# ScalarE copies the whole accumulator of an MLP feature block, and VectorE adds its halves in SBUF

## The chip, the core and the metric

The kernel runs on one NeuronCore of a Trainium2 chip. The metric is device time in microseconds (us) of one execution. Five engines work in parallel, each through its own instruction stream in order: TensorE (PE in the profile; its weight loads stand apart as PEld), VectorE (DVE), ScalarE (ACT), GpSimd (POOL) and SyncE (SP), which here issues the DMAs. They wait for one another by semaphores. Matmuls write to PSUM, which has eight banks of 512 f32 per partition; everything else lies in SBUF.

## The reference, cut to what matters

Two decoder layers over 256 tokens of width 2048, each with a mixer and a squared-ReLU MLP of width 8192, all in f32:

```python
def squared_relu_mlp(h, w1, w2):
    return jnp.square(jax.nn.relu(h @ w1)) @ w2

for layer in range(DEPTH):            # DEPTH = 2
    h = rms_norm(x, norm_mix[layer])
    x = x + mixer(h)                  # layer 0: MLA and mLSTM; layer 1: dilated attention
    x = x + squared_relu_mlp(rms_norm(x, norm_mlp[layer]), mlp_w1[layer], mlp_w2[layer])
return rms_norm(x, norm_final)
```

The change touches the middle of the MLP: the values of `h @ w1` on their way from PSUM to the ReLU.

## The kernel before, in words

**Three products for one.** Every f32 operand is split into a high part `hi` in the matmul format f32r and a low part `lo`, the rest. A product is `hi*hi + hi*lo + lo*hi`. Weights come by DMA in pieces of 512 KB (`load`, L118 to L128) and are split in `halves` (L130): ScalarE rounds them to `wh` (L135), VectorE subtracts to `wl` (L136). There are four raw buffers, four `wh` and four `wl`.

**Feature blocks.** In the first MLP product (`mm_feats`, L158) the weights are the stationary operand and the activations move. A tile `T` holds its two parts side by side, 256 tokens of `hi` and 256 of `lo`. So one matmul over 512 columns (L164) gives `wh*hi` in the left half of a PSUM bank and `wh*lo` in the right half, and a second one over 256 columns (L168) adds `wl*hi` to the left half. At the end of a feature block (128 features, 16 + 16 matmuls) the two halves of the bank have to be added. That is what `both` does (L282 to L286): ScalarE copies the right half to an SBUF tile `bt`, then VectorE adds it to the left half, which it reads from PSUM. Only when VectorE has read it is the bank free.

**After the sum.** `evac_h` (L1021) goes on from `both`: ScalarE applies ReLU (L1028) and squares (L1030 or L1039). For the first ten blocks of a quarter (`c < SEVEN`, `c` counting pairs) the squares of a pair of blocks go to a tile `hp`, VectorE makes three sums of it (L1041 to L1043), and ScalarE and VectorE split that into `pt` (L1045, L1046), the operand of a product scheme with seven multiplications for eight. For the other six, `ht` is split by `split_to` (L300, L301).

**The order of the MLP.** The 8192 features go in four quarters of 16 blocks. The first eight blocks of a layer run in pairs and rotate through the four accumulator banks. The other 56 run one at a time, all of them in bank 3 (`blocks`, L1083, `bank=3`, `kt=8`), so a block can't begin before the block before it has left the bank. To bridge that, `woven` (L443) puts steps of the second MLP product between the blocks: ten steps of `steps_seven`, alternately `go_a` (9 matmuls of 512 columns, L215) and `go_b` (12 of them, L235), go with eight blocks, so that one step, here and there two, stands between two blocks. Such a stretch of eight blocks comes seven times a layer, 14 times in all, and is followed by steps of `eight` (L248), second-product matmuls alone. A step of `go_a` also costs VectorE sums of weights (`ta`, `tb`, L225 to L228) beside the splitting.

**Who sets the order.** The source order is a priority. When the program is built, a planner gives each engine its sequence: it runs through the program with modelled durations, and an instruction whose inputs or buffers aren't ready there lets later ones pass on its engine. On the chip the sequence of each engine is fixed. The sequence of the changed program is planned anew.

Of the kernel before, what the change touches and what calls it, by code (L numbers as in the profile page):

```python
# [9 lines left out]
F32 = mybir.dt.float32  # L10
FR = mybir.dt.float32r
AF = mybir.ActivationFunctionType
OP = mybir.AluOpType

P = 128
S = 256
# [53 lines left out]
def trunk(ctx: ExitStack, tc: tile.TileContext, plan, a, c_first, c_even, c_odd, out):  # L70
    nc = tc.nc
# [192 lines left out]
    def steps_feats(Ts, w, c0, evac, n=256, name="f", kt=4, bank=None):  # L264

        box = {}
        groups = [range(i, i + kt) for i in range(0, len(Ts), kt)]

        def make(gi, g):
            def go():  # L270
                if gi == 0:
                    box["a"] = [acc(f"{name}{f}", bank) for f in range(n // P)]
                hi, lo = weights(w, g[0], kt, c0, n)
                mm_feats(box["a"], [Ts[k] for k in g], hi, lo, gi == 0, gi == len(groups) - 1)
                if gi == len(groups) - 1:
                    for f in range(n // P):
                        evac(f, box["a"][f])
            return go

        return [make(gi, g) for gi, g in enumerate(groups)]  # L280

    def both(pool, out, ac, name):  # L282

        t = pool.tile([P, S], F32, name=f"bt_{name}", tag="bt", bufs=2)
        nc.scalar.activation(t, ac[:, S:], AF.Copy)
        nc.vector.tensor_add(out, ac[:, :S], t)  # L286
# [10 lines left out]
    def split_to(T, src, scale=None):  # L297

        if scale is None:
            nc.scalar.activation(T[:, 0, :], src, AF.Copy)  # L300
            nc.vector.tensor_tensor(T[:, 1, :], src, T[:, 0, :].bitcast(F32), OP.subtract)  # L301
        else:
            nc.scalar.activation(T[:, 0, :], src, AF.Copy, scale=scale)
            nc.vector.scalar_tensor_tensor(T[:, 1, :], src, scale, T[:, 0, :].bitcast(F32),
                                           OP.mult, OP.subtract)
# [120 lines left out]
    def run(*streams):  # L426
        for st in streams:
            for go in st:
                go()
# [13 lines left out]
    def woven(main, side):  # L443

        done = 0
        for i, go in enumerate(main):
            want = -(-(i + 1) * len(side) // len(main))
            run(side[done:want])
            done = want
            go()  # L450
# [563 lines left out]
    def mlp(layer, norm, nxt):  # L1014
        st = ExitStack()
        sm = st.enter_context(tc.tile_pool(name=f"mlp{layer}", bufs=1))
        X = Late(norm.T)
        scale = {}
        NF = FF // NQ // P

        def evac_h(H):  # L1021
            def make(c):
                box = {}

                def go(f, ac):
                    u = sm.tile([P, S], F32, name="hu", tag="hu", bufs=2)
                    both(sm, u, ac, "h")
                    nc.scalar.activation(u, u, AF.Relu)  # L1028
                    if c >= SEVEN:
                        nc.scalar.activation(u, u, AF.Square)  # L1030
                        H[2 * c + f] = sm.tile([P, 2, S], FR, name="ht", tag="ht", bufs=2 * (NF // 2 - SEVEN))
                        split_to(H[2 * c + f], u)
                        return
                    if f == 0:
                        box["r"] = sm.tile([P, 8, P], F32, name="hp", tag="hp", bufs=2)
                    r = box["r"]
                    dst = r[:, 1:3, :] if f == 0 else r[:, 0:4:3, :]
                    v = u.rearrange("p (b t) -> p b t", b=NB)
                    nc.scalar.activation(dst, v, AF.Square)  # L1039
                    if f == 1:  # L1040
                        nc.vector.tensor_tensor(r[:, 4:6, :], r[:, 1:3, :], r[:, 2:4, :], OP.subtract)  # L1041
                        nc.vector.tensor_tensor(r[:, 6, :], r[:, 5, :], r[:, 1, :], OP.subtract)
                        nc.vector.tensor_tensor(r[:, 7, :], r[:, 0, :], r[:, 6, :], OP.add)  # L1043
                        pt = sm.tile([P, 2, 8, P], FR, name="pt", tag="pt", bufs=SEVEN)
                        nc.scalar.activation(pt[:, 0], r, AF.Copy)  # L1045
                        nc.vector.tensor_tensor(pt[:, 1], r, pt[:, 0].bitcast(F32), OP.subtract)  # L1046
                        H[2 * c], H[2 * c + 1] = (pt, 0), (pt, 1)
                return go
            return make

        def early_y(c):
            def go(m1, m5, m6, m7):
                def add(b, j, src):
                    v = x[b][c + j]
                    nc.vector.scalar_tensor_tensor(v, src, scale["s"][:, b:b + 1], v, OP.mult, OP.add)

                p = sm.tile([P, 512], F32, name="yp", tag="yp", bufs=1)
                q = sm.tile([P, 512], F32, name="yq", tag="yq", bufs=1)
                nc.scalar.activation(p, m1, AF.Copy)
                add(0, 0, m1)  # L1060
                nc.vector.tensor_add(p, m6, p)
                nc.vector.tensor_add(q, m7, p)
                nc.vector.tensor_sub(p, m5, p)
                add(1, 0, q)
                nc.vector.tensor_sub(q, m5, q)
                add(0, 1, p)
                add(1, 1, q)
            return go

        def late_y(c):  # L1070
            def go(cc):
                for b, j in ((1, 1), (1, 0), (0, 1), (0, 0)):
                    v = x[b][c + j]
                    nc.vector.scalar_tensor_tensor(v, cc[b, j], scale["s"][:, b:b + 1], v, OP.mult, OP.add)
            return go

        def evac_y(c):
            def go(ac):
                for b in range(NB):
                    nc.vector.scalar_tensor_tensor(x[b][c], ac[b], scale["s"][:, b:b + 1], x[b][c], OP.mult, OP.add)  # L1080
            return go

        def blocks(q, H):  # L1083

            ev = evac_h(H)

            def block(i):
                def go():
                    run(steps_feats(X, ("mlp_w1", layer, 0), q * (FF // NQ) + i * P,
                                    lambda f, ac: ev[i // 2](i % 2, ac), n=P, name="h", kt=8, bank=3))  # L1090
                return go

            ev = [ev(c) for c in range(NF // 2)]
            return [block(i) for i in range(NF)], ev

        H = [None] * NF
        hs, ev = blocks(0, H)
        steps = steps_feats(X, ("mlp_w1", layer, 0), 0, ev[0], name="h")
        run(steps[:3])
        norm.turn(3)  # L1100
        run(steps[3:])
        norm.close()
        scale["s"] = norm.inv_var()
        for c in range(1, NF // 4):
            run(steps_feats(X, ("mlp_w1", layer, 0), c * 256, ev[c], name="h"))
        for q in range(NQ):
            last = q == NQ - 1
            wq = ("mlp_w2", layer, q * (FF // NQ))
            seven, eight = steps_seven(sm, H, list(range(SEVEN)), wq, 0, early_y(0), late_y(0))
            woven(hs[NF // 2:], sum(seven, []))  # L1110
            run(*eight)
            if last and nxt is None:
                finish(H, wq, evac_y, scale, sm)
                break
            pairs = list(range(3 if last else SEVEN))
            seven, eight = steps_seven(sm, H, pairs, wq, 1024, early_y(2), late_y(2))
            if last:
                nxt.stats(0)
                nxt.stats(1)
                steps = sum([a + b for a, b in zip(seven, eight)] + eight[len(seven):], [])  # L1120
                run(steps[:-1], [lambda: nxt.turn(0)], steps[-1:], [lambda: nxt.turn(1)])
                break
            H = [None] * NF
            hs, _ = blocks(q + 1, H)
            sv = sum(seven, [])
            woven(hs[:NF // 2], sv)
            run(*eight)
        if nxt is not None:
            nxt.stats(2)
            nxt.stats(3)  # L1130
        return st
# [63 lines left out]
```

## Time and profile before

| what | value |
|---|---|
| median of 3 runs | 2154.32 us (2150.76 to 2155.19) |
| the profiled execution's own time | 2148.98 us |
| its span, first to last instruction | 2147.1 us |
| granted TensorE clock, mean over the span | 0.999 of full speed |
| instructions | 29491 |

The span is the time on the chip from the first to the last instruction, and the execution's own time lies 1.88 us above it. In the rows further down, times are in us from the span's start unless marked ns. "L164" is a line of the kernel, `h<-T,wh` says what is written from what, x8 is a count, and `[0.39 <-DVE hu L286]` means that the engine sat idle for 0.39 us before and that this instruction ended it. The end of a matmul is modelled, so two neighbouring matmuls overlap in the profile: their pace is the distance of their starts.

### The profile page before, as it was taken

The page shows a single profiled execution, that of the slowest core. Times are in us where ns is not written, and L with a number is a line of the kernel's source. Part 1 is how long each engine was busy: PE and PEld are TensorE (multiplying, and loading weights), DVE is VectorE, ACT ScalarE, POOL GpSimd, SP SyncE. Part 2 cuts the span into 40 slices and gives each one's busy share as a digit, 9 for nine tenths or more (in the row PEclk, how much of TensorE's full clock was granted, in tenths as well). Part 3 has the DMA queues.
Part 4 walks back from the last instruction along what each step waited for, and adds up shares of the span by engine and source line. Part 5 has one row for each costly group of instructions (what it writes and reads, how often), then busy time and mean ns, then how long its engine had stood idle before and what let it go on. Part 6 is the DMA issues. An engine that isn't in the chain of part 4 may idle for free. (4 is left out here: it accounts for less than half of the span.)

```text
span 2147.1 us, 29491 instructions
## 1 busy us (share of the span) xinstructions
PE 2116.2 (99%) x10995; PEld 1808.9 (84%) x10995; DVE 1667.3 (78%) x2346; ACT 1249.1 (58%) x1851; POOL 5.6 (0%) x12
## 2 busy tenths in 40 slices
PE   9999999999999999999999999999999999999998
PEld 8998888888888888888888888888888888888887
DVE  5678556878978888998877667557888889888975
ACT  6676445666665665666544544556656656566653
POOL 0000000000000000000000000000000000000000
PEclk9999999999999999999999999999999999999999
DMA  8554555555555555565555555455556556556664
GB/s 296 170 175 145 166 179 177 185 197 187 198 191 197 193 187 200 189 197 195 195 195 170 179 171 176 160 188 174 190 191 198 194 196 195 198 188 195 211 207 141
DMA packets 115279, 404.51 MB, mean 188 GB/s; under 512 B 12928, under 2 KB 13568, under 8 KB 115136
## 3 DMA queue, kind: packets, MB, share of 16 engines
q1 hardware_dynamic: 114624, 401.07, 56.7%
q8 instruction: 86, 1.41, 0.3%
q0 software_dynamic: 368, 1.51, 0.3%
q14 instruction: 57, 0.47, 0.1%
q10 hardware_dynamic: 144, 0.06, 0.0%
HBM read 400.49 MB, written 2.10 MB: 187 GB/s over the span
## 5 line engine op out<-in xcount | busy, mean ns | idle before, releaser
L136 DVE TENSOR_TENSOR wl<-wr,wh 128x1024 fp32r<-128x1024 f32 (+4 forms) x769 | 876.5, 1146 | 352.4 <-ACT wh L135 343.2
L135 ACT ACTIVATE wh<-wr 128x1024 fp32r<-128x1024 f32 (+4 forms) x769 | 763.2, 996 | 585.9 <-PE h L164 154.7
L164 PE MATMUL h<-T,wh 128*128 128x512 f32 x2048 | 518.1, 395 | 15.2 <-DVE hu L286 14.3
L164 PEld LDWEIGHTS h<-T,wh 128*128 128x128 f32 x2048 | 370.6, 188 | 107.4 <-DVE hu L286 37.3
L168 PEld LDWEIGHTS h<-T,wl 128*128 128x128 f32 x2048 | 279.2, 190 | 20.3
L168 PE MATMUL h<-T,wl 128*128 128x256 f32 x2048 | 285.3, 282 | 0.0
L154 PE MATMUL yc<-wh,ht 128*128 128x512 f32 x360 | 140.3, 390 | 0.0
L155 PE MATMUL yc<-wl,ht 128*128 128x512 f32 x360 | 140.2, 389 | 0.0
L156 PE MATMUL yc<-wh,ht 128*128 128x512 f32 x360 | 140.1, 389 | 0.0
L1028 ACT ACTIVATE hu<-hu 128x256 f32<-128x256 f32 x128 | 52.6, 415 | 109.8 <-DVE hu L286 109.8
L155 PE MATMUL ym<-wl,pt 128*128 128x512 f32 x292 | 114.5, 392 | 0.0
L154 PE MATMUL ym<-wh,pt 128*128 128x512 f32 x292 | 114.5, 392 | 0.0
L156 PE MATMUL ym<-wh,pt 128*128 128x512 f32 x292 | 113.6, 389 | 0.0
L225 DVE TENSOR_TENSOR ta<-wr,wr 128x1024 f32<-128x1024 f32 x73 | 89.2, 1222 | 30.6 <-DMA wr<-in_mlp_w 30.3
L154 PE MATMUL o<-wh,M 128*128 128x512 f32 x256 | 102.3, 399 | 0.0
L156 PE MATMUL o<-wh,M 128*128 128x512 f32 x256 | 99.8, 390 | 0.0
L155 PE MATMUL o<-wl,M 128*128 128x512 f32 x256 | 99.7, 389 | 0.0
L135 ACT ACTIVATE wh<-tb 128x1024 fp32r<-128x1024 f32 x73 | 76.9, 1053 | 35.5 <-DVE tb L228 35.2
L135 ACT ACTIVATE wh<-ta 128x1024 fp32r<-128x1024 f32 x73 | 77.0, 1055 | 30.4 <-DVE ta L225 30.2
L155 PE MATMUL yc<-wl,pt 128*128 128x512 f32 x235 | 91.8, 390 | 0.0
L154 PE MATMUL yc<-wh,pt 128*128 128x512 f32 x235 | 91.7, 390 | 0.0
L156 PE MATMUL yc<-wh,pt 128*128 128x512 f32 x235 | 91.6, 390 | 0.0
(314 smaller groups left out, 3343.0 us busy)
## 6 DMA issues: line engine op xcount, KB each, us to landing
wr<-in_mlp_w SPq DMA_DIRECT2D x512, 512.0 KB, 3.6
wr<-in_od_w_qkv SPq DMA_DIRECT2D x96, 512.0 KB, 4.2
wr<-in_ev_w_in SPq DMA_DIRECT2D x32, 512.0 KB, 3.5
wr<-in_ev_w_out SPq DMA_DIRECT2D x32, 512.0 KB, 3.4
wr<-in_od_w_out SPq DMA_DIRECT2D x32, 512.0 KB, 3.5
wr<-in_ev_w_in SPq DMA_DIRECT2D x24, 344.0 KB, 3.1
wr<-in_ev_w_in SPq DMA_DIRECT2D x15, 364.0 KB, 5.5
wr<-in_mla_w_ukv SPq DMA_DIRECT2D x8, 512.0 KB, 3.6
```

Source lines behind the costliest of these rows:

```text
L135: nc.scalar.activation(hi, raw, AF.Copy)
L136: nc.vector.tensor_tensor(lo, raw, hi.bitcast(F32), OP.subtract)
L154: nc.tensor.matmul(ac, xh, hi, start=first, stop=False)
L155: nc.tensor.matmul(ac, xh, lo, start=False, stop=False)
L156: nc.tensor.matmul(ac, xl, hi, start=False, stop=last)
L164: nc.tensor.matmul(acs[f], hi[:, j, f * P:(f + 1) * P], Ts[j].rearrange("p a t -> p (a t)"), start=first and j == 0, stop=False)
L168: nc.tensor.matmul(acs[f][:, :S], lo[:, j, f * P:(f + 1) * P], Ts[j][:, 0, :], start=False, stop=last and j == n - 1)
L225: nc.vector.tensor_tensor(ta, r0, r1[:, 0:1, :].to_broadcast([P, 2, 512]), OP.add)
L1028: nc.scalar.activation(u, u, AF.Relu)
```

## The change

In `evac_h`, ScalarE copies all 512 columns of the accumulator, both halves, to SBUF, and VectorE adds the two halves from there. The buffer `bt` is 512 f32 wide instead of 256 in the MLP. `both` stays as it is in the two mixers. Nothing else is edited.

```diff
                 def go(f, ac):
+                    t = sm.tile([P, 512], F32, name="bt_h", tag="bt", bufs=2)
+                    nc.scalar.activation(t, ac, AF.Copy)
                     u = sm.tile([P, S], F32, name="hu", tag="hu", bufs=2)
-                    both(sm, u, ac, "h")
+                    nc.vector.tensor_add(u, t[:, :S], t[:, S:])
                     nc.scalar.activation(u, u, AF.Relu)
```

## Rows read from the trace of the kernel before

**Rows 1.** The page's first part: busy time, share of the span, instructions.

```profile
PE 2116.2 (99%) x10995; PEld 1808.9 (84%) x10995; DVE 1667.3 (78%) x2346; ACT 1249.1 (58%) x1851; POOL 5.6 (0%) x12
```

**Rows 2.** Waits, whole span: who waited for whom: us in total, times, longest.

```profile
ACT hu L1028 <- DVE hu L286: 109.8, 104, 2.4
...
PEld h L164 <- DVE hu L286: 37.3, 55, 1.4
...
PE h L164 <- DVE hu L286: 14.3, 34, 1.0
...
PE c L154 <- ACT wh L135: 4.3, 1, 4.3
```

**Rows 3.** Timeline of PE in one stretch: start, us, what.

```profile
1932.63 0.39 PE L156 MATMUL ym<-wh,pt 128*128 128x512 f32 x1
1933.57 1.21 PE L164 MATMUL h<-T,wh 128*128 128x512 f32 x4 [0.56 <-DVE hu L286]
...
1941.80 0.39 PE L156 MATMUL yc<-wh,pt 128*128 128x512 f32 x1
1942.33 0.98 PE L164 MATMUL h<-T,wh 128*128 128x512 f32 x3
...
1948.03 0.40 PE L154 MATMUL ym<-wh,pt 128*128 128x512 f32 x1
...
1950.78 0.39 PE L154 MATMUL yc<-wh,pt 128*128 128x512 f32 x1
1951.56 2.14 PE L164 MATMUL h<-T,wh 128*128 128x512 f32 x8 [0.39 <-DVE hu L286]
1954.47 2.00 PE L164 MATMUL h<-T,wh 128*128 128x512 f32 x8
...
1976.85 0.39 PE L156 MATMUL ym<-wh,pt 128*128 128x512 f32 x1
1977.54 0.73 PE L164 MATMUL h<-T,wh 128*128 128x512 f32 x2 [0.29 <-DVE hu L286]
```

**Rows 4.** Timeline of ACT and DVE ahead of the third of those block starts.

```profile
1947.71 1.07 ACT L1045 ACTIVATE pt<-hp 128x1024 fp32r<-128x1024 f32 x1 [1.31 <-DVE hp L1043]
...
1948.68 1.05 ACT L135 ACTIVATE wh<-wr 128x1024 fp32r<-128x1024 f32 x1
...
1949.62 0.36 ACT L285 ACTIVATE bt_h<-h 128x256 f32<-128x256 f32 x1
...
1949.95 1.22 DVE L136 TENSOR_TENSOR wl<-wr,wh 128x1024 fp32r<-128x1024 f32 x1
...
1951.09 0.42 DVE L286 TENSOR_TENSOR hu<-h,bt_h 128x256 f32<-128x256 f32 x1
```

**Rows 5.** Groups by line and shape: count | busy us, mean ns | idle before.

```profile
L285 ACT ACTIVATE bt_h<-h 128x256 f32<-128x256 f32 x128 | 46.5, 370 | 4.5 <-PE h L168 4.5
L1059 ACT ACTIVATE yp<-ym 128x512 f32<-128x512 f32 x15 | 9.0, 597 | 2.5 <-PE ym L156 2.5
L286 DVE TENSOR_TENSOR hu<-h,bt_h 128x256 f32<-128x256 f32 x128 | 52.8, 418 | 1.4 <-ACT bt_h L285 1.3
L1041 DVE TENSOR_TENSOR hp<-hp 128x256 f32<-128x256 f32 x40 | 16.8, 419 | 1.7 <-ACT hp L1039 1.7
L1061 DVE TENSOR_TENSOR yp<-ym,yp 128x512 f32<-128x512 f32 x15 | 10.2, 681 | 0.0
```

**Rows 6.** Chain that ended last, in that stretch: start, us, what.

```profile
1933.21 5.62 DMA wr<-in_mlp_w
...
1938.85 1.24 DVE ta L225
...
1951.09 0.43 DVE hu L286
...
1951.56 2.14 PE h L164 x8
```

**Rows 7.** Windows: that stretch; then the sum of the two MLPs: busy us.

```profile
1941.40:2012.80 71.40, 70.58 (x353) 59.19 (x352) 66.05 (x82) 43.99 (x60) 0.58 (x1) 1.00 0.63 201
...
sum 1286.00, PE 1270.81 PEld 1071.24 DVE 1095.85 ACT 790.13 POOL 1.11; mean PE 635.41 PEld 535.62 DVE 547.92 ACT 395.07 POOL 0.55
```

## The prediction

> **What bounds the kernel now.** I read the page's first part, then the waits, then one stretch of the MLP in the timeline, then the chain and the windows. TensorE is busy for 2116.2 of the span's 2147.1 us [rows 1], so only the time in which it stands or runs below its pace can be won. The waits name one large loser: the first matmul of a feature block waits for VectorE's sum `hu` (L286), 14.3 us in 34 waits, and its weight load does so 55 times [rows 2]. In both MLPs together TensorE stands idle for 1286.00 - 1270.81 = 15.2 us [rows 7], so nearly all idle time there is this wait. It is the wait for bank 3: the next block can't start until VectorE has read the left half of the old one.
>
> What a wait really costs is more than the waits view says, because a matmul's end is modelled. In [rows 3] the reader is to see starts. The last matmul ahead of the third block start begins at 1950.78. Thirteen begin between 1948.03 and 1950.78, so the pace is 2.75 / 12 = 0.23 us and the block could begin at 1951.01. It begins at 1951.56: 0.55 us lost, where the view counts 0.39, so 0.16 more than shown. The first eight matmuls then take 2.14 us, the next eight 2.00: 0.14 us for the restart. By the same subtraction the four waits of this stretch lose 0.71, 0.30, 0.55 and 0.46 us.
>
> Over the kernel: 14.3 us shown, and 34 x 0.16 = 5.4 us not shown. The 55 - 34 = 21 waits that only the weight load shows lose between nothing and 0.16 us each, 0 to 3.4 us. The restart adds 0.14 us for 34 to 55 waits, 4.8 to 7.7 us. That is 24.5 to 30.8 us, **about 28 us** that bank 3 costs now and the most that the change can win.
>
> Why is `hu` late? ScalarE's copy `bt_h` is done at 1949.98, but VectorE is in a `wl` that began at 1949.95, and `hu` starts at 1951.09, ends at 1951.51, and the block begins 0.05 us later [rows 4]. The right half has long been copied; the bank is held for VectorE's place in its queue.
>
> **The change part by part.**
>
> *The copy grows from 256 to 512 columns.* It took 370 ns; a 512-column copy from PSUM by ScalarE takes 597 ns (L1059) [rows 5]. That is 0.227 us more, 128 times, 29.1 us of ScalarE work. ScalarE is busy for 790.13 of 1286.00 us in the MLPs [rows 7], so the work as such fits. Behind the copy on its queue stands the ReLU, which waits for VectorE anyway: 109.8 us in 104 waits, 1.06 us each [rows 2]. Those waits stay, they only begin later. I cost the longer copy at nothing but its own delay of the bank.
>
> *VectorE's add reads SBUF alone.* The row for such an add, both inputs in one SBUF tile, is L1041: 419 ns against 418 now [rows 5]. I take no gain. [...]
>
> *The bank comes free at the copy's end, not at the add's.* At the third start of [rows 3] the copy begins at 1949.62, would end at 1950.22 and release the bank at 1950.27, 1.29 us earlier than today's 1951.56. Alone, that wait is gone with 0.74 us to spare.
>
> *What is late next.* The waits of a stretch add up, and the copy isn't free to move. Without the first three waits and their two restarts TensorE would reach the third start 0.71 + 0.30 + 0.55 + 0.28 = 1.84 us earlier, at 1949.72. But the copy stands behind `pt`, which waited for VectorE's `hp` sums, and a `wh` [rows 4], and the chain runs from a DMA issued at 1933.21 through VectorE work to 1951.09 [rows 6]. That chain is not shortened, so the third start comes at 1950.27 at best: 1.29 us are won there and part of the wait stays. The fourth wait goes whole, 0.46 + 0.14. So the stretch wins 1.29 + 0.60 = 1.89 of its 2.58 us (2.02 and four restarts), 73%. With the same share of 28 us the kernel wins **20 us**. The bounds are 31 us (all of it) and, with the copies later than in this stretch, a few us.
>
> *Weights.* A faster TensorE asks for weights up to 2 us earlier in a stretch of 71.40 us. In the MLPs it never waited for one: the only wait of TensorE on a weight half is at the start of the even layer, 4.3 us [rows 2]. VectorE, the busier helper, has 71.40 - 66.05 = 5.35 us free in the stretch [rows 7], so I cost this at nothing. If that cover were gone, it would eat the gain.
>
> *DMA and SBUF.* No DMA is added or moved in the source; `bt` takes 2 KB more per partition, which costs no time.
>
> The sum against the profiled execution: span 2147.1 - 20 = 2127, own time 2148.98 - 20 = 2129. The median of the runs is 5.3 us above that execution, so the forecast is 2154.3 - 20 = **2134 us**.
>
> **The rivals.**
>
> *The planner takes most of it back: 2147 us.* After the second block start the source has one `go_a`, 9 matmuls, before the next block, but 13 stand there [rows 3]: the planner, finding bank 3 held, let four of the next step pass. If it now sees the bank free earlier and puts the block right behind the nine, TensorE arrives 4 x 0.23 = 0.92 us earlier at a copy that is no earlier. In 14 stretches that gives back 13 us of 20. For it: the planner's durations aren't the chip's, and the copy comes late just there. Against it: the copy's place may move too.
>
> *VectorE is the next bound: 2152 us.* From 1938.85 to 1951.5 the chain is VectorE almost without a break [rows 6]. If TensorE now catches up with the `wl` parts, each wait for a bank becomes a wait for a weight. Some 2 us, within 0.2% of before; 0.2%, 4.3 us, is about what a measurement of this kernel can tell from no change. Against it: 5.35 free us a stretch [rows 7], and no such wait so far [rows 2].
>
> *ScalarE is late instead, and it is slower: 2170 us.* The bank now hangs on ScalarE alone. Its place is the three block starts of a stretch with a `go_a` of nine matmuls ahead: 9 x 0.23 = 2.1 us, less the last block's modelled tail, some 1.9 us from a block's end. With two `wh` copies of 1.05 us [rows 4] queued ahead of the copy, the bank comes free 0.1 + 2.1 + 0.6 = 2.8 us after the end: 0.9 us of waiting and 0.14 of restart, 42 times, 44 us against today's 28, so 16 us lost. It decides from a release 1.9 + 28 / 42 - 0.14 = 2.4 us after a block's end. For it: at the third start a `pt` and a `wh` already stand ahead of the copy. Against it: it has 39% of the MLPs free [rows 7]. [...]
>
> **How the numbers follow.** Forecast 0.60 (2126 to 2142 by itself), planner 0.20, VectorE 0.10, ScalarE 0.08, and 0.02 for the whole 28 us and more, 2124. Faster by over 0.2%: 0.60 + 0.20 + 0.02 = 0.82; within: 0.10; slower: 0.08. The range goes from all of the loss won, 2124, to beyond the planner's case, 2150.
>
> **What would show it.** Right, if the waits list hardly a TensorE wait on `hu`, what is left names `bt_h`, mostly at the third start of a stretch, the copy takes 0.60 us and the add 0.42, and TensorE's idle time in the MLPs drops from 15 us to under 5. The planner's case shows 9 matmuls instead of 13 ahead of that start and waits of about 1 us on `bt_h`; VectorE's shows waits on `wl`; ScalarE's shows `wh` copies between a block's end and its `bt_h`. I am wrong if the waits on `hu` are gone and the span is not shorter by more than 10 us.

## The result and the profile after

| | before | after |
|---|---|---|
| median of the runs side by side | 2153.6 us (4 runs, 2150.76 to 2155.19) | 2129.21 us (4 runs, 2125.78 to 2130.89) |
| the profiled execution: own time, span | 2148.98, 2147.1 us | 2129.08, 2127.3 us |

The ratio is 0.9886 with a 95% interval of 0.9869 to 0.9903: the kernel is faster, by 24.4 us in the medians and by 19.8 us between the two profiled spans.

The page's first part after, to be held against [rows 1]:

```profile
PE 2106.3 (99%) x10995; PEld 1811.5 (85%) x10995; DVE 1663.6 (78%) x2346; ACT 1275.7 (60%) x1851; POOL 5.6 (0%) x12
```

ScalarE works 26.6 us more, VectorE about as much as before, and TensorE's busy time has fallen by 9.9 us for the same 10995 matmuls. Parts of a late start count as busy in it: up to 0.16 us of the modelled end ahead of it (0.39 us less the pace of 0.23), and about 0.11 us of restart behind it. With 36 late starts fewer, as counted below, that is an estimate of up to 9.7 us.

The waits after (who waited for whom: us in total, times, longest):

```profile
ACT hu L1030 <- DVE hu L1029: 118.2, 113, 2.4
...
DVE ta L225 <- DMA wr<-in_mlp_w: 64.8, 40, 3.2
...
PEld h L164 <- ACT bt_h L1027: 10.5, 17, 1.1
...
PE h L164 <- ACT bt_h L1027: 3.4, 8, 0.7
...
PE yc L154 <- DVE x L1076: 1.2, 2, 1.0
```

TensorE's 34 waits for `hu` with 14.3 us [rows 2] are now 8 waits for the copy `bt_h` with 3.4 us. ScalarE's ReLU still waits for VectorE, a little longer than in [rows 2], and TensorE doesn't wait for it.

The two groups that the change edits (count | busy us, mean ns | idle before), and then the sum of windows over the two MLPs:

```profile
L1027 ACT ACTIVATE bt_h<-h 128x512 f32<-128x512 f32 x128 | 73.6, 582 | 0.9 <-PE h L168 0.9
...
L1029 DVE TENSOR_TENSOR hu<-bt_h 128x256 f32<-128x256 f32 x128 | 52.9, 419 | 0.0
```

```profile
sum 1265.00, PE 1260.04 PEld 1073.08 DVE 1090.08 ACT 815.88 POOL 1.11; mean PE 630.02 PEld 536.54 DVE 545.04 ACT 407.94 POOL 0.55
```

TensorE's idle time in the MLPs is 1265.00 - 1260.04 = 5.0 us, against 15.2 in [rows 7].

**Counted by starts.** A block start is late by its distance from the start of the matmul before, less that matmul's pace of 0.227 us. Over the whole trace of before, 51 block starts are late by more than 0.03 us, 23.1 us together, and the matmul after each loses 5.6 us more in all: 28.7 us. After the change 15 are late, 6.1 and 1.65 us: 7.8. The difference is 20.9 us, 1.1 more than the change of the span. In this count a restart is 0.11 us, where the prediction took 0.14. This count is used for the experiments too.

**The same stretch after.** Starts are numbered here as in [rows 3], whose first is the second block of its stretch; the last of the four in [rows 3] is the sixth by this count. The timeline of all engines, at what is the second and the third start:

```profile
1921.47 1.23 DVE L225 TENSOR_TENSOR ta<-wr,wr 128x1024 f32<-128x1024 f32 x1 [1.99 <-DMA wr<-in_mlp_w]
...
1922.73 1.06 ACT L135 ACTIVATE wh<-ta 128x1024 fp32r<-128x1024 f32 x1 [1.72 <-DVE ta L225]
...
1923.22 0.39 PE L156 MATMUL yc<-wh,pt 128*128 128x512 f32 x1
...
1923.69 0.58 ACT L1027 ACTIVATE bt_h<-h 128x512 f32<-128x512 f32 x1
...
1924.32 2.12 PE L164 MATMUL h<-T,wh 128*128 128x512 f32 x8 [0.71 <-ACT bt_h L1027]
...
1930.24 0.58 ACT L1027 ACTIVATE bt_h<-h 128x512 f32<-128x512 f32 x1
...
1931.47 1.06 ACT L1047 ACTIVATE pt<-hp 128x1024 fp32r<-128x1024 f32 x1 [0.65 <-DVE hp L1045]
...
1931.86 0.39 PE L156 MATMUL ym<-wh,pt 128*128 128x512 f32 x1
...
1932.09 1.98 PE L164 MATMUL h<-T,wh 128*128 128x512 f32 x8
```

At the third start the copy now stands **ahead of** `pt`, where it stood behind it and a `wh` in [rows 4]. It is done at 1930.82, and the block begins at the pace, 0.23 us behind the matmul ahead of it, and waits for nothing. So it is in 12 of the 14 stretches. In the first stretch of each layer the copy still stands behind `pt` and a `wh`, and there the third start is late, by 0.62 and 0.21 us. At the second start of the stretch shown the copy stands behind the `wh` of `ta`, which waited for VectorE's `ta`, which waited for a DMA; the block begins 0.87 us late, the worst of the 15. TensorE's own sequence differs in 14 places and by one pattern: of the 13 matmuls ahead of the third start, four (three `ym` and a `yc`) now come behind the block.

### The profile page after: what moved, and what is told of

The parts are those of the page before. It is cut to its first block, busy times and chain, and to the rows that moved or that the text cites. A ratio compares the mean times of both kernels' runs of the same rounds, so it can differ in the third digit from the quotient of the medians.

```text
span 2127.3 us, 29505 instructions
## 1 busy us (share of the span) xinstructions
PE 2106.3 (99%) x10995; PEld 1811.5 (85%) x10995; DVE 1663.6 (78%) x2346; ACT 1275.7 (60%) x1851; POOL 5.6 (0%) x12
## 4 chain that ended last, share of the span: by engine, by line
PE 89%; DVE 4%; DMA 4%; issue 1%; ACT 1%; SPq 0%; POOLq 0%; DVEq 0%; POOL 0%; ACTq 0%
PE h L164 19%; PE h L168 10%; PE yc L154 5%; PE yc L155 5%; PE yc L156 5%; DMA wr<-in_mlp_w 4%; PE k L164 3%; PE o L154 3%; PE o L156 3%; PE o L155 3%; PE q L164 3%; PE ym L155 3%; PE ym L154 3%; PE ym L156 3%; PE v L154 2%; PE v L156 2%
## 5 line engine op out<-in xcount | busy, mean ns | idle before, releaser
L164 PE MATMUL h<-T,wh 128*128 128x512 f32 x2048 | 512.9, 392 | 3.7 <-ACT bt_h L1027 3.4
L164 PEld LDWEIGHTS h<-T,wh 128*128 128x128 f32 x2048 | 373.7, 188 | 82.5 <-ACT bt_h L1027 10.5
L225 DVE TENSOR_TENSOR ta<-wr,wr 128x1024 f32<-128x1024 f32 x73 | 89.2, 1222 | 65.0 <-DMA wr<-in_mlp_w 64.8
```

Source lines behind the costliest of these rows:

```text
L164: nc.tensor.matmul(acs[f], hi[:, j, f * P:(f + 1) * P], Ts[j].rearrange("p a t -> p (a t)"), start=first and j == 0, stop=False)
L225: nc.vector.tensor_tensor(ta, r0, r1[:, 0:1, :].to_broadcast([P, 2, 512]), OP.add)
```

## Experiments

**1. Is it the early release?** The first kernel has the change's long copy but lets VectorE read the left half from PSUM, so that the bank is held until the add.

```diff
-                    nc.vector.tensor_add(u, t[:, :S], t[:, S:])
+                    nc.vector.tensor_add(u, ac[:, :S], t[:, S:])
```

> ScalarE still copies all 512 columns, but VectorE adds the left half from PSUM, so the bank is held to the add as before; everything else is as after the change. Theory (the gain is the bank's earlier release): no gain is left; the copy is 0.22 us longer where VectorE waits for it, so 2150 to 2160 us, and the waits of TensorE name the sum hu again, 12 to 18 us. Rival (the gain comes from the sequences that the planner made anew, or from the add reading SBUF): 2125 to 2140 us, with few waits on hu.

Measured: 2152.57 us (10 runs) beside 2151.73 (13 runs), ratio 0.9999 (0.999 to 1.0009). Its waits:

```profile
PEld h L164 <- DVE hu L1029: 28.3, 46, 1.4
...
PE h L164 <- DVE hu L1029: 10.3, 26, 1.0
```

51 starts are late, as many as before. They lose 22.9 us where those lost 28.7, but the kernel isn't faster for it: the weight loads of the second product have new waits, 4.8 us for `wl` and 4.3 for `wh`. All of the gain is in what this kernel leaves out, the release ahead of the add.

**2. The release, or the new sequences?** Since everything was planned anew, the gain could be the plan's. Two kernels hold the sequences of TensorE, VectorE and ScalarE by dependencies that order without a semaphore (`_pin`, its body left out here): the change in the sequences of before, and the code of experiment 1 in the sequences of the change.

```diff
+        _pin(tc, nc)
```

> The change, with TensorE, VectorE and ScalarE held to the sequences of the kernel before, instruction for instruction: only the release and the longer copy are new. Theory (the release is the gain, as the prediction summed it with the order unchanged): 20 us of the 28 are won, 2126 to 2137 us, the waits of TensorE name the copy, mostly at the third start of a stretch, where the copy stands behind pt. Rival (the new sequences are the gain): 2145 to 2155 us.

> The bank held to VectorE's add from PSUM, as before the change, but all three engines held to the sequences of the kernel after the change. Theory: in these sequences the add stands behind more wl than before, and in the trace after the change it ends behind the next block's start in 70 of 100 cases, by 80 us in all; each delay of TensorE gives VectorE time, so not all of that: 2165 to 2210 us, slower than before the change. Rival (the new sequences are the gain): 2125 to 2140 us.

Measured: the change in the old sequences 2127.41 us, ratio 0.9887 (0.9869 to 0.9904); the held bank in the new ones 2155.88 us (10 runs), ratio 1.0018 (1.0008 to 1.0029). The waits of the first, then of the second:

```profile
PE h L164 <- ACT bt_h L1027: 4.2, 8, 0.8
```

```profile
PE h L164 <- DVE hu L1029: 22.8, 38, 1.4
```

The same stretch again, in the change with the old sequences; the second start, then the third:

```profile
1920.92 1.06 ACT L135 ACTIVATE wh<-ta 128x1024 fp32r<-128x1024 f32 x1 [1.80 <-DVE ta L225]
1921.88 0.58 ACT L1027 ACTIVATE bt_h<-h 128x512 f32<-128x512 f32 x1
1922.52 2.11 PE L164 MATMUL h<-T,wh 128*128 128x512 f32 x8 [0.79 <-ACT bt_h L1027]
...
1928.52 1.06 ACT L1047 ACTIVATE pt<-hp 128x1024 fp32r<-128x1024 f32 x1 [1.31 <-DVE hp L1045]
1929.49 1.04 ACT L135 ACTIVATE wh<-wr 128x1024 fp32r<-128x1024 f32 x1
1930.44 0.58 ACT L1027 ACTIVATE bt_h<-h 128x512 f32<-128x512 f32 x1
1930.96 0.39 PE L154 MATMUL yc<-wh,pt 128*128 128x512 f32 x1
1931.19 1.07 PE L164 MATMUL h<-T,wh 128*128 128x512 f32 x4
```

The time of this kernel is as expected, the place of its waits isn't. The copy stands behind `pt` and a `wh` at the third start, with 13 matmuls ahead, as in [rows 4], and yet none of the 14 third starts is late. The 11 late ones are five second starts (3.1 us) and six sixth ones (2.7 us).

| ratio to before | bank held to the add | bank free at the copy's end |
|---|---|---|
| sequences of before | 1 | 0.9887 |
| sequences of the change | 1.0018 | 0.9886 |

The upper left cell is the kernel before itself, with its copy of 256 columns; experiment 1 showed that the longer copy, held, costs nothing that can be measured. The early release is worth the same 1.1 to 1.3% in either plan, and the plan by itself is worth nothing, or 0.2% the wrong way. That loss has the sign that I expected and is far smaller, 2155.88 us for 2165 to 2210: the late starts rose from 23.1 to 30.6 us, not by the 80 us of late sums that I counted. I read that as time that VectorE gains in every pause of TensorE; no run shows it by itself.

**3. Which engine copies?** VectorE copies the whole bank in ScalarE's place; and, last of all the runs, VectorE copies only the right half and adds the left from PSUM, so that the bank is held.

```diff
-                    nc.scalar.activation(t, ac, AF.Copy)
+                    nc.vector.tensor_copy(t, ac)
```

> VectorE instead of ScalarE copies all 512 columns, then adds in SBUF. Theory (what matters is which queue the bank hangs on): the release goes back to VectorE's queue and VectorE gets 128 x 0.6 to 0.7 us = 77 to 87 us more work, 5 us in each stretch that has 5 us to spare: slower than before the change, 2160 to 2200 us, waits of TensorE on the copy and on wl. Rival (any copy of the whole accumulator will do, since the add is what holds the bank): 2125 to 2145 us. [...]

```diff
-                    both(sm, u, ac, "h")
+                    t = sm.tile([P, S], F32, name="bt_h", tag="bt", bufs=2)
+                    nc.vector.tensor_copy(t, ac[:, S:])
+                    nc.vector.tensor_add(u, ac[:, :S], t)
```

> The kernel before, but VectorE instead of ScalarE copies the right half to SBUF, and then adds the left half to it from PSUM. The bank is held until the add, as before, but its release now needs one place in one queue instead of a place on ScalarE and then one on VectorE. VectorE has some 50 us more work (128 copies of about 0.4 us), so the bank is busy for about 0.8 us after VectorE takes it. One theory reads the gain of VectorE's whole copy (2138 us) as the gain of having one queue ahead of the release: then this kernel is close to it, 2137 to 2146 us, few waits of TensorE on the sum, and VectorE stands idle ahead of the copy, waiting for a block's end. The rival reads it as the gain of freeing the bank ahead of the add: then TensorE waits for the sum about as often as in the kernel before (34 times and 14 us, or more, since VectorE has more to do), and the time is 2150 to 2165 us.

Measured: 2138.27 us, ratio 0.9934 (0.9919 to 0.9949), a miss, since I expected a loss, and the rival's time; and 2163.89 us, ratio 1.006 (1.0043 to 1.0077), again the rival's time. VectorE's copy in the first:

```profile
L1027 DVE COPY bt_h<-h 128x512 f32<-128x512 f32 x128 | 87.1, 685 | 32.3 <-PE h L168 32.1
```

The waits of the second:

```profile
PE yc L154 <- ACT wh L135: 8.3, 14, 0.7
PE ym L154 <- ACT wh L135: 7.6, 26, 0.7
...
PE h L164 <- DVE hu L1029: 0.7, 3, 0.4
```

Neither theory had the place of that second loss. By the view TensorE hardly waits for `hu`; by the count of starts 38 blocks are still late, by 5.9 us together, against 23.1 before. TensorE's sequence is changed all through the MLPs, with other numbers of second-product matmuls ahead of the blocks, and now those matmuls wait for `wh`, 15.9 us. I take it that the planner found the bank late and let them pass, so that the loss is paid under another name; that is argued, not shown. One queue instead of two isn't what made VectorE's whole copy fast: with one queue and a held bank the kernel is slower than before. The four kernels agree with one another:

| us | bank held to the add | bank free at the copy's end | release worth |
|---|---|---|---|
| ScalarE copies | 2152.6 | 2129.2 | 23 |
| VectorE copies | 2163.9 | 2138.3 | 26 |

Each was planned anew and timed beside its own runs of before, so these are not single edits; by the ratios the release is worth 24 and 27 us. But it is worth that whoever copies, and the copy on VectorE costs 9 to 11 us (10 to 13 by the ratios). One f32 copy of a whole bank takes VectorE 685 ns and ScalarE 582.

**4. The copy's length and its place.** First the copy done twice (0.6 us more on ScalarE and until the release), then the copy kept behind the `pt` of the pair before it, as in [rows 4] (of that edit the main lines).

```diff
                     nc.scalar.activation(t, ac, AF.Copy)
+                    nc.scalar.activation(t, ac, AF.Copy)
```

> ScalarE makes the same copy twice in a row, so each release comes about 0.5 us later and ScalarE works 64 us more. Theory (what counts is the release against TensorE's arrival, 15 block starts being late now and some ten more with under 0.5 us to spare): 24 late starts, about 10 us more waiting: 2135 to 2145 us. Rival (ScalarE's own time is short, so that each copy costs what it takes): 112 x 0.5 = 56 us more, 2175 to 2190 us. Third way (the late starts are set by something else): no change, 2125 to 2133 us.

```diff
-                    nc.scalar.activation(t, ac, AF.Copy)
+                    if "pt" in pinned:
+                        with tc.issue_after(pinned["pt"]):
+                            nc.scalar.activation(t, ac, AF.Copy)
...
-                        nc.scalar.activation(pt[:, 0], r, AF.Copy)
+                        pinned["pt"] = nc.scalar.activation(pt[:, 0], r, AF.Copy).ins
```

> Each copy is queued on ScalarE behind the last pt of the pair before, the place that it had at the third start of a stretch before the change; otherwise as after the change. Theory (the planner put TensorE's block behind nine matmuls, as the rival of the prediction had it, and it was paid for by moving the copy ahead of pt): the third start becomes late by about 1 us in most of the 14 stretches: 8 to 14 us back, 2137 to 2143 us, waits on the copy 10 to 20 us in the view of weight loads. Rival (the copy's place on ScalarE does not matter, since the 1.9 us of nine matmuls cover it): 2125 to 2133 us.

Measured: 2135.53 us, ratio 0.993 (0.9908 to 0.9951), 6.3 above the change and inside what was expected; and 2133.37 us, ratio 0.9919 (0.9901 to 0.9938), 4.2 above it and just above the rival's range, with the profiled run at 2139.5, inside the theory's range and 6 to 7 us above the other three. A wait of the first kernel, then one of the second:

```profile
PE h L164 <- ACT bt_h L1028: 5.9, 7, 1.7
```

```profile
PE h L164 <- ACT bt_h L1030: 11.4, 18, 1.1
```

So 75 us of additional ScalarE work cost 6 us (9 by the ratios): its time isn't short. There are 24 late starts, as expected; they lose 12.4 us, 4.6 more than after the change. The second kernel has TensorE's sequence of the change, and the place of a copy of 0.6 us among its neighbours costs 4 us by the medians (7 by the ratios), where the intervals still touch, and more in the profiled run (22 late starts, 15.0 and 2.4 us). All 14 third starts are late in that trace, 10.4 us of the 15.0, as the theory had it: nine matmuls don't cover a copy behind `pt`.

**5. What holds the rest?** In the change's trace above, VectorE's `ta` waits for weights. So I gave `r1`, one of the two pieces of `ta`, a fifth raw buffer (in the room of `yp` and `yq`, which go to the buffer of `tb`), in the change and in the kernel before.

```diff
-        raw = wpool.tile([P, kt, n], F32, name=f"wr{n_w[0]}", tag="raw", bufs=4)
+        raw = (pool or wpool).tile([P, kt, n], F32, name=f"wr{n_w[0]}", tag="raw", bufs=1 if pool else 4)
...
-                r1 = load(w, [(2 * k, c + 512, 512), (2 * k + 1, c, 512)], (2, 512))
+                r1 = load(w, [(2 * k, c + 512, 512), (2 * k + 1, c, 512)], (2, 512), pool)
...
-                p = sm.tile([P, 512], F32, name="yp", tag="yp", bufs=1)
-                q = sm.tile([P, 512], F32, name="yq", tag="yq", bufs=1)
+                pq = sm.tile([P, 2, 512], F32, name="yp", tag="tb", bufs=1)
+                p, q = pq[:, 0, :], pq[:, 1, :]
```

> After the change, with a fifth raw weight buffer in the MLP: the second piece of each go_a step has a buffer of its own (paid for by laying yp and yq into tb's buffer). Theory (the starts that are still late hang on a copy that stands on ScalarE behind wh of ta, which waits for ta, which waits for that piece's DMA): the piece lands earlier, VectorE's waits for DMA ahead of ta fall from 65 us to under 30, the late starts (6.1 us by the paces, 1.7 us of restarts) shrink by half or more: 2121 to 2127 us. Rival (the copies are late by ScalarE's order itself): no change, 2127 to 2132 us.

> The kernel before with the same fifth buffer. Theory (its block starts hang on VectorE's queue, which is full whenever the DMA lands): little, 2145 to 2153 us. Rival (the DMA was the root of the late sums too, by the chain that ran from a DMA to the third start): 10 us or more, 2130 to 2142 us.

Measured: with the change 2137.9 us, ratio 0.993 (0.9916 to 0.9945), a miss: 8.7 us slower than the change alone. Without it 2139.63 us, ratio 0.9942 (0.9925 to 0.9958), the rival's number. VectorE's waits for `ta` didn't fall in either (71.2 and 61.8 us). But the weight does land earlier, and VectorE, which reaches `ta` earlier too, only waits longer for it. The first start and the `ta` after it, in the change and then in the change with the buffer:

```profile
1915.14 1.98 PE L164 MATMUL h<-T,wh 128*128 128x512 f32 x8
...
1921.47 1.23 DVE L225 TENSOR_TENSOR ta<-wr,wr 128x1024 f32<-128x1024 f32 x1 [1.99 <-DMA wr<-in_mlp_w]
```

```profile
1921.76 1.98 PE L164 MATMUL h<-T,wh 128*128 128x512 f32 x8
...
1926.64 1.23 DVE L225 TENSOR_TENSOR ta<-wr,wr 128x1024 f32<-128x1024 f32 x1 [3.92 <-DMA wr<-in_mlp_w]
```

In the median of the 14 stretches `ta` begins 3.9 us behind the first start instead of 5.8 with the change, and 3.0 instead of 4.6 in the kernel before. With it the late second starts fall from eight (3.7 us) to two (0.65 us). So the buffer does there what it was made for, and the loss is elsewhere. The timeline of ScalarE and TensorE shows where:

```profile
1937.43 1.06 ACT L1047 ACTIVATE pt<-hp 128x1024 fp32r<-128x1024 f32 x1 [1.10 <-DVE hp L1045]
...
1937.98 0.39 PE L156 MATMUL ym<-wh,pt 128*128 128x512 f32 x1
...
1938.40 1.04 ACT L135 ACTIVATE wh<-wr 128x1024 fp32r<-128x1024 f32 x1
...
1939.35 0.58 ACT L1027 ACTIVATE bt_h<-h 128x512 f32<-128x512 f32 x1
...
1939.98 2.11 PE L164 MATMUL h<-T,wh 128*128 128x512 f32 x8 [1.61 <-ACT bt_h L1027]
```

This is the third start with nine matmuls ahead and the copy behind `pt` and a `wh`: the block is 1939.98 - 1938.21 = 1.77 us late. It is so, by 1.68 to 1.78 us, in seven of the 14 stretches (12.3 us of the 14.2 that its late starts lose). The kernel before with this buffer wins 13 us. Both its weights and its sequences differ from those of before, and no run parts the two. The sequences of the first can be judged, since its code also ran in those of the second:

```diff
+        _pin(tc, nc)
```

> The change with the fifth raw buffer, all three engines held to the sequences that the planner gave the kernel before with that buffer (which came to 2140 us against 2153). Theory (what a sequence is worth and what the release is worth add up): its late sums, 15.3 us by the paces and 3.2 of restarts, go for the most part: 2120 to 2128 us, at or below the change. Rival (once the copy frees the bank the rest is the copy's place behind wh of ta): 2129 to 2136 us.

Measured: 2126.4 us, ratio 0.9881 (0.9864 to 0.9898): 11.5 us faster than the same code in its own plan (10.5 by the ratios), as the theory had it, and not to be told from the change. 15 of its starts are late, by 5.0 us. Beside the kernel before with the buffer, which has the same sequences, the release is worth 13 us, less than in experiment 3: that kernel loses only 18.5 us to late starts.

The last two put the copy ahead of the `wh` of `ta`, without and with the fifth buffer.

```diff
-                h1, l1 = halves(ta, pool, "t", 3)
+                with tc.issue_after(newest["bt"]):
+                    h1, l1 = halves(ta, pool, "t", 3)
...
-                    nc.scalar.activation(t, ac, AF.Copy)
+                    newest["bt"] = nc.scalar.activation(t, ac, AF.Copy).ins
```

> After the change, with the splitting of ta (wh on ScalarE, and only that) queued behind the newest copy of an accumulator. Theory (15 starts are late because that splitting stands ahead of the copy and waits): the copy runs at the block's end, all late starts but a few go: 2121 to 2126 us. Rival (the weights are the next bound: the splitting, begun up to 2 us later, makes TensorE wait for wl or wh of ta instead): 2127 to 2140 us, with waits of ym on wl.

> The fifth raw buffer and the splitting of ta behind the newest copy together. If both theories hold, there is nothing more to win than the 8 us that the late starts cost: 2120 to 2125 us, hardly a wait on the copy. If the pin costs and the buffer wins, it lies between the two, 2123 to 2132 us.

Measured: 2138.22 us, ratio 0.9933 (0.9919 to 0.9948), the rival's time; and 2132.21 us, ratio 0.9906 (0.9891 to 0.9921), just above the range of its second case. Waits of the first:

```profile
PEld ym L155 <- DVE wl L136: 18.4, 44, 1.7
...
PE ym L155 <- DVE wl L136: 3.7, 6, 1.3
...
PE h L164 <- ACT bt_h L1030: 2.7, 4, 1.0
```

TensorE's waits for the copy shrink, from 3.4 to 2.7 us, and waits for `wl` appear, 3.7 us and 18.4 in the view of weight loads: what the copy gains, the weights of `ta` more than lose. No kernel here is clearly faster than the change.

## Why the prediction was right, and where it wasn't

**The loss of 28 us** was right: 28.7 by the count of starts. **The cause** was right, and experiments 1 and 2 show it: with the bank held there is no gain in either plan, with it released early the same gain in both.

**The prices of the edits** were right. The copy takes 582 ns where I took 597, and its work cost nothing that experiment 1 could measure (ratio 0.9999). The add takes 419 ns from SBUF alone where it took 418 with its left half in PSUM, so it gained nothing, as predicted. A block begins 0.05 us after the copy's end, as assumed (1923.69 + 0.58 to 1924.32).

**The share of 73%** came out to the digit, 20.9 of 28.7 us, but by another way. The step that failed is "what is late next": that the wait at the second start goes whole, and that it partly stays at the third, where the copy stands behind `pt` and its chain isn't shortened. Of the 14 third starts all were late before (4.9 us), two are after (0.8 us). What stays is mostly at the second start, behind the `wh` of `ta` (8 of the 15, 3.7 of 6.1 us), and at five of the sixth starts (1.6 us).

The new plan moved the copy ahead of `pt` in 12 stretches, but that isn't why the step failed: in experiment 2 the old sequences keep it behind `pt`, and no third start is late there either. What I didn't look at was the copy's place at the second start. The trace of before has it:

```profile
1940.11 1.06 ACT L135 ACTIVATE wh<-ta 128x1024 fp32r<-128x1024 f32 x1 [0.52 <-DVE ta L225]
1941.08 0.36 ACT L285 ACTIVATE bt_h<-h 128x256 f32<-128x256 f32 x1
```

A copy of 597 ns begun at 1941.08 frees the bank at 1941.73, 0.60 us ahead of the old start at 1942.33. The prediction let TensorE arrive there 0.71 + 0.14 + 0.30 = 1.15 us earlier, so by its own way of reckoning the wait would already stay at the second start, on the `wh` of `ta`.

That the two remainders are alike in size is chance. The stretch that the sum was made from shows it: between the starts of its first and its last block it became 1.16 us shorter, not 1.89, and the other 13 made up for it. And a copy behind `pt` can cost time, with nine matmuls ahead instead of 13: in experiment 5 a plan puts it there, up to 1.78 us late.

**The planner's rival** was right in what the planner does, nine matmuls for thirteen in all 14 stretches. Its price of 13 us is about right where the copy stays behind `pt`: experiment 4 makes that case, and its third starts lose 10.4 us and 1.5 of restarts in the profiled run. After the change the copy moved with the matmuls in 12 stretches, as the sentence against the rival allowed. Experiment 2 gives the new sequences no price that can be measured.

**Weights at nothing** was right for the change: TensorE has a new wait of 1.2 us, for VectorE's `x`, and none for `wl`. VectorE's wait for `ta`'s weights doubled, 30.3 us in the trace before to 64.8, but it costs only where a `wh` and a copy stand behind it (eight second starts, 3.7 us late together). Experiment 5 shows `wl` as the next bound once the copy goes first (waits of 3.7 us, and 18.4 in the view of weight loads).

**ScalarE late** didn't come: at 60% busy it has room, even for two copies (75 us more of its work cost 6.3 us). What counts is the place on its queue (third starts up to 1.78 us late in experiment 5, with the copy behind `pt` and a `wh`).

**The sum.** Span 2127.3 against 2127, own time 2129.08 against 2129. The forecast of the median, 2134, was 4.8 us too high, and the step is the last one: I added the 5.3 us by which the median of before lay above its profiled execution. After the change the profiled execution lies at the median. In later comparisons before had medians of 2151.2 to 2152.9, so part of the 24.4 us is the scatter of four runs.

## What to carry to other kernels

When a producer waits for a buffer, ask which instruction releases it and which queues that instruction stands in: a longer copy on the engine whose place comes early can be cheaper than a short one whose release hangs on a second engine (here 2129.2 us against 2153.6). Count such a stall by the starts of the matmuls, not by the waits alone (here 28.7 us against 14.3). If a planner lays out the queues anew, read the place of the releasing instruction in the new plan, and try the edit in the old order too; otherwise the plan and the edit can't be told apart. And look that place up at every start that waits, not at one: here what stayed of the stall was at another start than the one reckoned.

## What was not expected

Sequences alone move this kernel by more than 10 us at the same work: 11.5 us between two plans of the code with the fifth buffer. And a stall can change its name: with VectorE copying half the bank, 0.7 us of waits for the bank stand beside 15.9 for `wh`, in the slowest kernel of all. A longer wait need not be a later one either: the fifth buffer brought `ta` forward (3.9 us behind the first start instead of 5.8), while VectorE's waits for its weights grew from 64.8 to 71.2 us. Of the chip's own timing nothing surprised; in experiment 4 a second copy of the same bank took 596 ns, the first 583:

```profile
L1028 ACT ACTIVATE bt_h<-h 128x512 f32<-128x512 f32 x128 | 75.3, 596 | 2.6
...
L1027 ACT ACTIVATE bt_h<-h 128x512 f32<-128x512 f32 x128 | 73.8, 583 | 2.6 <-PE h L168 2.6
```
